# Moving the last output projection of an RWKV-7 layer behind the operands of the next stage

## The chip, the cores and the metric

The kernel runs on one core of a Trainium2 chip. The metric is the device time of one execution in microseconds (us). A core has five engines that run their own instruction streams side by side: TensorE (PE, matrix products, with the weight load shown apart as PEld), VectorE (DVE), ScalarE (ACT), GpSimd (POOL) and SyncE (SP, which here only issues transfers). PE writes its results to PSUM; all other data of the engines lies in SBUF, and transfers (DMAs) carry it to and from the chip's memory (HBM). A DMA is issued from the queue of SP, ACT or POOL. Each engine and each queue works in its own fixed order; an instruction that waits holds up what stands behind it.

## The reference

One inference step of a two-layer trunk with width 1024, for 1024 prompt tokens and 8 x 16 sample tokens (1152 columns in all). Layer 0 is RWKV-7 time mixing and a SwiGLU FFN, layer 1 is chunk-band attention with shared keys and values and a SwiGLU FFN. What matters here is the end of the time mixing of layer 0 and the entry into its FFN:

```python
y = ((y - mu) * lax.rsqrt(var + LNX_EPS)).reshape(bsz, t, d)      # per head of 64
y = y * ln_w + ln_b
y = y + bonus                                                     # r, k, v of the same token
out = (y * g) @ w_o                                               # the output projection
...
x = x + gt_m[:, None, :] * out                                    # the residual
h = modulate(rms_norm(x, p['norm_ffn'][l]), sh_f, sc_f)           # the FFN's input
x = x + gt_f[:, None, :] * swiglu(h, w_gate, w_up, w_down)
```

The norm's factor of a token, rsqrt(mean of x squared), needs all 1024 features of the new x, so all eight output tiles of the projection.

## The kernel before, in words

Data lies with features on the 128 partitions (8 feature tiles) and tokens along the free axis. Every float32 product is done as three products of a high and a low part: `split` (L268, L269) makes them, the high part with a copy on ACT, the low part with a subtraction on DVE; `mm3` issues the three matmuls (all by `mm`, L139).

Layer 0 works on three blocks of 384 tokens (`NB`, `TB`). Each block's projections run for all features; then its tokens go through the recurrence in *windows* of 128 tokens, three per block, each in two halves `hf` of four feature tiles. Window w of block b is (w, hf) with b = w // 3. Windows 6, 7 and 8 belong to block 2; window 8 holds the sample tokens. `win_run` computes a half window, `win_y` collects its result in one PSUM bank, and `win_post` (L1047 on) ends it: loads of the gate (tile gl, L1052) and of the bonus (bv, L1054), the copy out of PSUM (y, L1056), the per-head norm by two matmuls with constants and ACT's Square (L1059), Ln (L1063) and Exp (L1064), three DVE steps (L1065, L1069, L1070), and a store to the DRAM tensor yg of the block from ACT's queue (L1071). gl, bv and y have one buffer each.

`outproj(b)` is the output projection of a block. It loads the block's yg feature by feature on SP's queue (tile mr, two buffers, L1166), splits it into 16 operand tiles (tag mx), and then for each of 8 output tiles takes a weight tile (`wunit`: load of rw_o, two buffers, on POOL's queue by `wload` at L256, then a split of 1024 columns into whi and wlo), runs 24 matmuls of 384 columns into one of two PSUM banks, adds the gated result to x (`residual`, L1151 to L1156), stores it to the DRAM tensor x1 (L1179) and adds its squares to a sum (`sq_add`, L306 and L307). At the end `sq_done` makes the factors (one matmul with ones, `rsqrt2`, L326 to L330), and they are stored to the DRAM tensor rr (L1182).

`layer0a` runs the windows of block 2 in the order (6,0) (6,1) (8,0) (7,0) (7,1) (8,1), two at a time, and beside them the projections of blocks 0 and 1. After the last window its pool of buffers is closed, and `outproj(2)` follows.

`dense` is the rest. It opens two pools where the windows' pool was: h0 (14 tiles of 1024 columns, tag h) and wq (16 tiles of 512 columns, tag w, and five, tag rq). The FFN's tokens are two groups, c = 0 (tokens 0 to 511, all from blocks 0 and 1) and c = 1 (tokens 512 to 1151, with all of block 2). A group's gate and up products use Strassen's scheme: `strassen_in` loads the factors (L1438) and the eight input tiles (L1262), applies norm and shift (`normed`, L349 and L350, for sample tokens L357 to L359), forms 16 sums of a half width (256 or 320 columns, `comb`, L1268, on GpSimd) and splits 28 half tiles. Its inputs for c = 0 lie for the time being in w tiles, those for c = 1 in a pool (tag e) that takes the place of the projection's operand tiles. `strassen_weights` loads four weight tiles into rq tiles, forms four sums (L1309 to L1312), and splits seven. `gate_up` multiplies, sums with DVE and GpSimd (L1338), and stores; `ffn` runs it for the first weight tile on c = 0 and on c = 1 apart, and for the 21 others on both.

The order of instructions on each engine is not written out by hand: the program is emitted in the order of the code, and a scheduler in the build simulates the program's time and puts each engine's and each queue's instructions in order by which can start, the earlier emitted first where several can. The order is fixed from then on. A tile in a newly opened pool waits for the older tiles that lay on its bytes, each tile by itself.

Of the kernel before, what the change touches and what calls it, by code (L numbers as in the profile page):

```python
# [17 lines left out]
TB = 384  # L18
# [123 lines left out]
class Trunk:  # L142
# [166 lines left out]
    def sq_done(self, st):  # L309
# [9 lines left out]
        r = self.ev("rms", 1)[:, :w]  # L319
# [726 lines left out]
    def win_post(self, w, hf, R):  # L1046
# [4 lines left out]
        gt = self.wt("gl", [128, 512], 1)  # L1051
        nc.sync.dma_start(gt.rearrange("p (f t) -> p f t", f=4), self.sp[b]["g"][:, wi, fs, :])  # L1052
        bv = self.wt("bv", [128, 512], 1)
        nc.sync.dma_start(bv.rearrange("p (f t) -> p f t", f=4), self.sp[b]["v"][:, wi, fs, :])  # L1054
        y = self.wt("y", [128, 512], 1)
# [15 lines left out]
        nc.scalar.dma_start(self.yg[b][:, fs, wi * 128:(wi + 1) * 128], y.rearrange("p (f t) -> p f t", f=4))  # L1071
# [85 lines left out]

    def outproj(self, b):
# [3 lines left out]
        hi, lo = [], []  # L1162
        for f in range(8):
            h, l = self.mtile(), self.mtile()
            t = self.mraw()
            nc.sync.dma_start(t, self.yg[b][:, f, :])  # L1166
            self.split(h, l, t)
            hi.append(h)
            lo.append(l)
# [12 lines left out]
        nc.sync.dma_start(self.rr[:, cols], self.sq_done(st))  # L1182

    def layer0a(self, ctx):
        self.yg = [self.dp.tile([128, 8, TB], F32, name=f"yg{b}") for b in range(NB)]
# [16 lines left out]
        def early():  # L1202
            yield from self.alternate(self.outproj(0), self.ada, 1, 1)
            yield from self.outproj(1)
        for _ in self.alternate(self.windows([divmod(int(x), 2) for x in '12 13 16 14 15 17'.split()]), early(), 1, 2):
            pass
        cw.close()
        for _ in self.outproj(2):
            pass
        self.wqueue = None  # L1210
# [5 lines left out]
    def wide_open(self, ctx, name):  # L1216
        self.wq = ctx.enter_context(self.tc.tile_pool(name="wq" + name, bufs=1, reuse_waits="tile"))
        self.rawtag = "h0"
        self.hw = ("w", "w", 16)
        self.halfraw = lambda: self.wq.tile([128, 512], F32, tag="rq", name=self.nm("rq"), bufs=5)  # L1220

# [33 lines left out]
    def strassen_in(self, B, x, r, A, sh0, c, X):  # L1255
# [4 lines left out]
        gp = nc.gpsimd  # L1260
# [162 lines left out]
    def dense(self, x2, x3, close):  # L1423
# [4 lines left out]
        with ExitStack() as ctx:  # L1428
            pool = lambda n, **k: ctx.enter_context(self.tc.tile_pool(name=n, bufs=1, reuse_waits="tile", **k))
            self.hps = {0: pool("h0")}  # L1430
            with ExitStack() as c2:
                self.wide_open(c2, "0")
# [3 lines left out]
                def part(c, temp):  # L1436
                    r, *X = [temp() for _ in range(9)]
                    nc.sync.dma_start(r, self.rr[:, self.cols(c)])  # L1438
                    return self.strassen_in(B, self.x1, r, A, 24, c, X)
# [513 lines left out]
```

## Time and profile before

| | |
|---|---|
| median of 3 runs | 3858.28 us (3854.87 to 3863.27) |
| the profiled execution | 3864.46 us |
| its span, first to last instruction | 3862.7 us |
| granted PE clock over the span | 0.932 of full speed |
| instructions | 72343 |

The profile belongs to one execution. Its times count from the span's start. A row of the order of time gives start, length, engine, line, operation, and the tiles as output<-input with their shapes; in brackets stands how long the engine was idle before it, and what ended that. Releasers are inferred from semaphores. A row of a group gives the number of instructions, their busy time in us, the mean of one in ns and the idle time before them. The clock that the throttle granted to PE is a share of full speed. The stretch that the change touches lies between about 1200 and 1400 us.

### The profile page before, as it was taken

Reading aid. Unit: us, or ns where it says so; the run is one execution under the profiler, and the core shown is the slowest. Engines: PE = TensorE matmul, PEld = TensorE weight load, DVE = VectorE, ACT = ScalarE, POOL = GpSimd, SP = SyncE. Lnnn points to the kernel's source line nnn. Section 1 sums busy time; section 2 is a strip of 40 time slices with the busy share of each in tenths; the row PEclk is TensorE's granted clock in tenths of the full one; section 3 lists DMA queues with packets and bytes.
Section 4 is the critical chain, followed back from the end, with each engine's and each line's share of the span. In section 5 each row is a group of like instructions: output and inputs, shape, how many; then the busy total and the mean of one; then the engine's idle time right before and its main releaser. Section 6 shows DMA issues by size and latency. Waiting matters only on the chain.

```text
span 3862.7 us, 72343 instructions
## 1 busy us (share of the span) xinstructions
PE 3540.6 (92%) x28614; PEld 3125.0 (81%) x28614; DVE 2291.8 (59%) x4420; ACT 1575.7 (41%) x2998; POOL 643.2 (17%) x564
## 2 busy tenths in 40 slices
PE   5889989989888699999999899789889799999999
PEld 4777778777666599999887879677777799999998
DVE  4666666765445764554456752666675764554567
ACT  5545646544223433333311353565654533333310
POOL 0000000000010364453000100000000254453000
PEclk8887998889798789999999999899999899999999
DMA  5775776776664412223755112454555322222521
GB/s 209 233 218 163 214 207 182 200 199 199 187 201 147 143 67 75 74 75 105 254 179 182 70 62 97 141 152 140 153 185 167 116 80 75 74 75 92 171 86 70
DMA packets 428963, 552.31 MB, mean 143 GB/s; under 512 B 128432, under 2 KB 296880, under 8 KB 424144
## 3 DMA queue, kind: packets, MB, share of 16 engines
q1 hardware_dynamic: 352640, 449.49, 36.4%
q0 software_dynamic: 21840, 79.31, 6.8%
q10 hardware_dynamic: 54144, 18.89, 2.1%
q8 instruction: 225, 3.69, 0.4%
q14 instruction: 114, 0.93, 0.1%
HBM read 413.42 MB, written 134.12 MB: 142 GB/s over the span
## 4 chain that ended last, share of the span: by engine, by line
PE 69%; DMA 9%; DVE 9%; issue 6%; ACT 5%; POOL 1%; SPq 1%; ACTq 0%; DVEq 0%; POOLq 0%
PE S L139 31%; PE PT L139 15%; PE acc L139 13%; PE st L139 3%; PE O L139 2%; PE G L139 1%; DVE h L269 1%; PE PT L1779 1%; PE aux L139 1%; DMA raw<-in_wada 1%; DMA TT<-Z 1%; DMA Z<-T 1%; DVE wlo L269 1%; PE Y L139 1%; ACT pts L1780 1%
## 5 line engine op out<-in xcount | busy, mean ns | idle before, releaser
L139 PE MATMUL S<-h,w 128*128 128x320 f32 (+1 forms) x4944 | 698.9, 300 | 18.2 <-DVE h L269 7.7
L139 PEld LDWEIGHTS S<-h,w 128*128 128x128 f32 x4944 | 676.8, 192 | 26.6 <-DVE h L269 12.8
L139 PE MATMUL acc<-mx,whi 128*128 128x384 f32 x1728 | 512.5, 374 | 41.8 <-ACT mx L268 20.2
L139 PE MATMUL S<-h,wh 128*128 128x320 f32 (+1 forms) x2844 | 529.8, 337 | 14.0 <-DVE h L1151 8.1
L139 PEld LDWEIGHTS S<-h,wh 128*128 128x128 f32 x2844 | 455.4, 189 | 70.6 <-issue 11.7
L139 PEld LDWEIGHTS acc<-mx,whi 128*128 128x128 f32 x1728 | 340.4, 205 | 74.1 <-ACT mx L268 23.9
L268 ACT ACTIVATE w<-rq 128x512 fp32r<-128x512 f32 x308 | 192.4, 629 | 503.5 <-PE S L139 203.1
L269 DVE TENSOR_TENSOR w<-rq,w 128x512 fp32r<-128x512 f32 x308 | 268.6, 875 | 199.5 <-ACT w L268 198.9
L139 PE MATMUL PT<-h,w 128*128 128x320 f32 (+1 forms) x2448 | 355.4, 300 | 14.1 <-ACT w L268 6.9
L139 PEld LDWEIGHTS PT<-h,w 128*128 128x128 f32 x2448 | 337.9, 192 | 17.8 <-ACT w L268 7.1
L139 PE MATMUL acc<-mx,wlo 128*128 128x384 f32 x864 | 318.8, 369 | 6.5 <-DVE wlo L269 6.5
L139 PE MATMUL PT<-h,wh 128*128 128x320 f32 (+1 forms) x1428 | 286.4, 344 | 10.8 <-DVE wh L269 3.9
L1338 POOL TENSOR_TENSOR t<-t,t 128x576 f32<-128x576 f32 (+1 forms) x132 | 216.5, 1641 | 417.0 <-ACT t L1345 295.3
L139 PEld LDWEIGHTS PT<-h,wh 128*128 128x128 f32 x1428 | 233.5, 190 | 41.7 <-issue 6.0
L269 DVE TENSOR_TENSOR wlo<-raw,whi 128x1024 fp32r<-128x1024 f32 x114 | 139.6, 1226 | 85.3 <-ACT whi L268 84.3
L139 PEld LDWEIGHTS acc<-mx,wlo 128*128 128x128 f32 x864 | 176.7, 205 | 16.3 <-DVE wlo L269 10.3
L269 DVE TENSOR_TENSOR h<-h,h 128x1024 fp32r<-128x1024 f32 (+4 forms) x112 | 122.9, 1111 | 89.9 <-ACT h L268 73.0
L268 ACT ACTIVATE wh<-rq 128x512 fp32r<-128x512 f32 x124 | 74.8, 625 | 242.8 <-PE S L139 160.7
L268 ACT ACTIVATE h<-h 128x1024 fp32r<-128x1024 f32 (+4 forms) x112 | 103.3, 935 | 168.1 <-DMA h<-sd 111.7
L268 ACT ACTIVATE whi<-raw 128x1024 fp32r<-128x1024 f32 x114 | 119.6, 1053 | 124.3 <-PE acc L139 78.9
L1338 DVE TENSOR_TENSOR t<-S,t 128x576 f32<-128x576 f32 (+1 forms) x116 | 86.4, 745 | 132.0 <-PE S L139 132.0
L1405 DVE TENSOR_TENSOR h<-h,S 128x640 f32<-128x640 f32 (+1 forms) x150 | 111.9, 750 | 78.8 <-PE S L139 78.7
(433 smaller groups left out, 5754.7 us busy)
## 6 DMA issues: line engine op xcount, KB each, us to landing
h<-in_wada SPq DMA_DIRECT2D x64, 512.0 KB, 6.4
rq<-in_wg SPq DMA_DIRECT2D x88, 256.0 KB, 2.6
rq<-in_wu SPq DMA_DIRECT2D x88, 256.0 KB, 2.6
rq<-in_wd SPq DMA_DIRECT2D x88, 256.0 KB, 3.0
raw<-in_wada POOLq DMA_DIRECT2D x32, 512.0 KB, 5.0
kc<-in_ck SPq DMA_DIRECT2D x16, 1024.0 KB, 5.0
vc<-in_cv SPq DMA_DIRECT2D x16, 1024.0 KB, 5.8
sd<-t SPq DMA_DIRECT2D x88, 160.0 KB, 1.9
```

What stands on the lines that cost most here:

```text
L139: return nc.tensor.matmul(out, lhsT, rhs, start=start, stop=stop)
L268: self.nc.scalar.activation(hi, x, AF.Copy)
L269: self.nc.vector.tensor_tensor(lo, x, hi, ALU.subtract)
L1338: eng.tensor_tensor(out, x, y, ALU.add)
L1405: nc.vector.tensor_tensor(y, y, d, ALU.add)
L1779: nc.tensor.transpose(pt[:, j * 128:(j + 1) * 128], P[:, j * 128:(j + 1) * 128], self.C("ident"))
L1780: nc.scalar.activation(pts[:, 0:nk * 128], pt[:, 0:nk * 128], AF.Copy)
```

## The change

- `win_post`: the half window (7, 1) takes its gl, bv and y from the ring TT (six buffers of the same size) instead of the three single buffers. The half windows (7, 1) and (8, 1) no longer store y to yg: each splits its four 128-column pieces directly into the columns of the operand tiles of `outproj(2)`.
- `last_in` and `out_in`: the operand tiles of `outproj(2)` are made once, right after `outproj(1)` or with the first of these two ends. Their loads go through `wload`, at that time on POOL's queue, and for features 4 to 7 only the first 128 of 384 columns (window 6) are loaded.
- `dense`: the operands of group c = 0 are emitted ahead of `outproj(2)`; `outproj(2)` then alternates with the making of the first FFN weight tiles, four steps to one.
- The norm factors of block 2 stay in an SBUF tile (r2, one of the five rq tiles); group c = 1 copies them from there with ACT, and loads only the 256 factors of block 1 from rr.
- In layer 0 the sums of `strassen_in` for both groups run on VectorE instead of GpSimd. Layer 1 keeps them on GpSimd.
- `wide_open` is divided, so that the pool wq can be open while `outproj(2)` still takes its raw weights from the projection's pool.

```diff
-    def sq_done(self, st):
+    def sq_done(self, st, r=None):
...
-        r = self.ev("rms", 1)[:, :w]
+        r = self.ev("rms", 1)[:, :w] if r is None else r
...
-        gt = self.wt("gl", [128, 512], 1)
+        new = lambda tag: self.wt(tag, [128, 512], 1)
+        if (w, hf) == (7, 1):
+            new = lambda tag: self.wt("TT", [128, 8, 64], 6).rearrange("p c t -> p (c t)")
+        gt = new("gl")
...
-        bv = self.wt("bv", [128, 512], 1)
+        bv = new("bv")
...
-        y = self.wt("y", [128, 512], 1)
+        y = new("y")
...
-        nc.scalar.dma_start(self.yg[b][:, fs, wi * 128:(wi + 1) * 128], y.rearrange("p (f t) -> p f t", f=4))
+        if hf == 1 and w > 6:
+            cs = slice(wi * 128, (wi + 1) * 128)
+            for f in range(4):
+                h, l = (t[4 + f][:, cs] for t in self.last_in())
+                self.split(h, l, y[:, f * 128:(f + 1) * 128])
+        else:
+            nc.scalar.dma_start(self.yg[b][:, fs, wi * 128:(wi + 1) * 128], y.rearrange("p (f t) -> p f t", f=4))
+
+    def last_in(self):
+
+        if not self.yin:
+            self.yin = self.out_in(2, self.wload, 128)
+        return self.yin
...
-    def outproj(self, b):
-
-        nc, pp = self.nc, self.pp
-        cols = slice(b * TB, (b + 1) * TB)
+    def out_in(self, b, load, n=TB):
+
         hi, lo = [], []
         for f in range(8):
             h, l = self.mtile(), self.mtile()
-            t = self.mraw()
-            nc.sync.dma_start(t, self.yg[b][:, f, :])
-            self.split(h, l, t)
+            m = TB if f < 4 else n
+            t = self.mraw()[:, :m]
+            load(t, self.yg[b][:, f, :m])
+            self.split(h[:, :m], l[:, :m], t)
             hi.append(h)
             lo.append(l)
+        return hi, lo
+
+    def outproj(self, b):
+
+        nc, pp = self.nc, self.pp
+        cols = slice(b * TB, (b + 1) * TB)
+        hi, lo = self.last_in() if b == 2 else self.out_in(b, nc.sync.dma_start)
...
-        nc.sync.dma_start(self.rr[:, cols], self.sq_done(st))
+        if b < 2:
+            nc.sync.dma_start(self.rr[:, cols], self.sq_done(st))
+        else:
+            self.r2 = self.halfraw()[:, :TB]
+            self.sq_done(st, self.r2)
...
             yield from self.outproj(1)
+            self.last_in()
...
         cw.close()
-        for _ in self.outproj(2):
-            pass
-        self.wqueue = None
...
-    def strassen_in(self, B, x, r, A, sh0, c, X):
+    def strassen_in(self, B, x, r, A, sh0, c, X, gp=None):
...
-        gp = nc.gpsimd
+        gp = gp or nc.gpsimd
...
                 def part(c, temp):
                     r, *X = [temp() for _ in range(9)]
-                    nc.sync.dma_start(r, self.rr[:, self.cols(c)])
-                    return self.strassen_in(B, self.x1, r, A, 24, c, X)
+                    if c:
+                        nc.sync.dma_start(r[:, 0:256], self.rr[:, 512:768])
+                        nc.scalar.activation(r[:, 256:640], self.r2, AF.Copy)
+                    else:
+                        nc.sync.dma_start(r, self.rr[:, self.cols(c)])
+                    return self.strassen_in(B, self.x1, r, A, 24, c, X, nc.vector)
...
+                W = []
+
+                def weights():
+                    for t in self.strassen_weights(0, 0, nc.vector):
+                        W.append(t)
+                        yield
                 for _ in part(0, lambda: self.wq.tile([128, 512], F32, tag="w", name=self.nm("x"), bufs=16)):
                     pass
-                W = list(self.strassen_weights(0, 0, nc.vector))
+                for _ in self.alternate(self.outproj(2), weights(), 4, 1):
+                    pass
+                self.wqueue = None
+                self.rawtag = "h0"
                 close()
```

More of the change, by code (lines that the diff above doesn't have):

```diff
@@ L1156, in residual @@
             nc.vector.tensor_tensor(out[:, n:], t, x[:, n:], ALU.add)
+    def out_in(self, b, load, n=TB):
+        hi, lo = [], []
+        for f in range(8):
+            h, l = self.mtile(), self.mtile()
+            m = TB if f < 4 else n
+            t = self.mraw()[:, :m]
+            load(t, self.yg[b][:, f, :m])
+            self.split(h[:, :m], l[:, :m], t)
+            hi.append(h)
+            lo.append(l)
+        return hi, lo
     def outproj(self, b):
@@ L1161, in outproj @@
         cols = slice(b * TB, (b + 1) * TB)
-        hi, lo = [], []
-        for f in range(8):
-            h, l = self.mtile(), self.mtile()
-            t = self.mraw()
-            nc.sync.dma_start(t, self.yg[b][:, f, :])
-            self.split(h, l, t)
-            hi.append(h)
-            lo.append(l)
+        hi, lo = self.last_in() if b == 2 else self.out_in(b, nc.sync.dma_start)
         st = self.sq_open()
@@ L1181, in outproj @@
             yield
-        nc.sync.dma_start(self.rr[:, cols], self.sq_done(st))
+        if b < 2:
[3 more added lines that the diff above has]
+            self.sq_done(st, self.r2)
     def layer0a(self, ctx):
+        self.yin = None
         self.yg = [self.dp.tile([128, 8, TB], F32, name=f"yg{b}") for b in range(NB)]
@@ L1207, in layer0a, with wq_open, wide_open @@
         cw.close()
-        for _ in self.outproj(2):
-            pass
-        self.wqueue = None
         ct.push(c1)
         return ct.close
-    def wide_open(self, ctx, name):
+    def wq_open(self, ctx, name):
         self.wq = ctx.enter_context(self.tc.tile_pool(name="wq" + name, bufs=1, reuse_waits="tile"))
-        self.rawtag = "h0"
         self.hw = ("w", "w", 16)
         self.halfraw = lambda: self.wq.tile([128, 512], F32, tag="rq", name=self.nm("rq"), bufs=5)
+    def wide_open(self, ctx, name):
+        self.wq_open(ctx, name)
+        self.rawtag = "h0"
     def wide_open2(self, ctx, name):
@@ L1431, in dense @@
             with ExitStack() as c2:
-                self.wide_open(c2, "0")
+                self.wq_open(c2, "0")
                 A = self.gain("nf0", 32)
@@ L1447, in done @@
                     yield from self.normed_split(c, *X[c], self.Ak, 96, *HK[c])
+                W = []
[3 more added lines that the diff above has]
+                        yield
                 for _ in part(0, lambda: self.wq.tile([128, 512], F32, tag="w", name=self.nm("x"), bufs=16)):
                     pass
-                W = list(self.strassen_weights(0, 0, nc.vector))
+                for _ in self.alternate(self.outproj(2), weights(), 4, 1):
+                    pass
+                self.wqueue = None
+                self.rawtag = "h0"
                 close()
```

## The prediction, on record before the changed kernel was run

> **What bounds the kernel now.** I read the page first, then the busy time by stage around the place that the change touches, then who waited there, then the instructions in order of time.
>
> ```profile
> span 3862.7 us, 72343 instructions
> PE 3540.6 (92%) x28614; PEld 3125.0 (81%) x28614; DVE 2291.8 (59%) x4420; ACT 1575.7 (41%) x2998; POOL 643.2 (17%) x564
> ```
>
> TensorE (PE) is busy for 92% of the span, so over the whole kernel only its idle stretches and its slow ones can be won. The view by stage shows one such place, about 130 us long (columns: the stretch, its length, then busy us and instructions of PE, of PE's weight load, of VectorE, ScalarE and GpSimd, then the granted clock, DMA share, GB/s).
>
> ```profile
> 1240.00:1262.00 22.00, 4.30 (x8) 1.05 (x6) 5.09 (x13) 3.40 (x7) 0.00 (x0) 0.55 0.24 71
> 1262.00:1316.00 54.00, 39.87 (x168) 35.94 (x168) 47.18 (x84) 29.17 (x59) 22.62 (x20) 0.80 0.47 155
> ...
> 1330.00:1372.00 42.00, 31.25 (x120) 24.63 (x119) 37.79 (x68) 21.52 (x46) 28.48 (x24) 0.63 0.23 80
> 1372.00:1400.00 28.00, 28.00 (x200) 28.00 (x201) 18.35 (x25) 11.00 (x20) 15.54 (x13) 0.94 0.29 98
> ```
>
> The first stretch is the end of the last two windows: every engine is nearly idle. The second is the last output projection (168 of its 192 matmuls; 24 ran earlier) together with the first group's operands: VectorE (DVE) is busy 47.18 of 54 us, and PE works at a granted clock of 0.80. The third is the second group's operands: DVE 37.79 of 42 us, PE at 0.63. From 1372 PE is dense. So this place is bound first by a chain of waits and then by DVE. The order of time shows the chain (start, length, engine, line, what; the idle time before it and its releaser in brackets), first PE, then ScalarE (ACT).
>
> ```profile
> 1238.83 1.30 PE L139 MATMUL Y<-XL,ssv 64*64 64x16 f32 x30
> ...
> 1261.97 1.33 PE L139 MATMUL acc<-mx,whi 128*128 128x384 f32 x3 [9.42 <-ACT mx L268]
> ```
>
> ```profile
> 1242.94 0.43 ACTq L1071 DMA_DIRECT2D yg<-y  x1
> 1247.06 0.60 ACT L1056 ACTIVATE y<-Y 128x512 f32<-128x512 f32 x1 [6.78 <-DMA yg<-y]
> ...
> 1256.59 0.37 ACTq L1071 DMA_DIRECT2D yg<-y  x1
> 1261.39 1.02 ACT L268 ACTIVATE mx<-mr 128x384 fp32r<-128x384 f32 x2 [7.46 <-DMA mr<-yg]
> ```
>
> Window 8's result is complete in PSUM at 1240.13 (1238.83 + 1.30), but its copy starts only at 1247.06, since window 7's end has the one buffer y until its store is out. The end itself then takes 9.5 us (1247.06 to the store at 1256.59), and another 5.4 us go by (1256.59 to 1261.97) while y is written to memory, read back and split.
>
> **The change part by part.**
>
> **(1) The last ends.** Window 7's end takes three buffers of another ring, so window 8's copy can follow its matmuls at 1240.2; both ends write their split straight into the projection's operand tiles. That removes two stores on ACT's queue and cuts four loads to a third of their columns.
>
> ```profile
> L269 DVE TENSOR_TENSOR h<-x,h 128x256 fp32r<-128x256 f32 x28 | 15.3, 574 | 2.0 <-ACT h L268 1.9
> ...
> L349 DVE SCALAR_TENSOR_TENSOR x<-x,mod,x 128x512 f32<-128x512 f32 x8 | 5.8, 749 | 2.2 <-DMA x<-x 2.2
> L307 DVE TENSOR_TENSOR sqa<-sqa,kk 128x384 f32<-128x384 f32 x7 | 5.6, 800 | 1.7 <-ACT kk L306 1.7
> ...
> L1156 DVE TENSOR_TENSOR e<-e,rr 128x128 f32<-128x128 f32 x8 | 2.3, 282 | 0.1
> ...
> L269 DVE TENSOR_TENSOR mx<-mr,mx 128x384 fp32r<-128x384 f32 x4 | 2.2, 557 | 5.4 <-ACT mx L268 5.4
> ```
>
> (DVE's groups from 1262 to 1322: busy us, mean ns, idle before.) In place of 4 splits of 384 columns, 2.2 us on DVE, stand 12 of 128, at 0.28 us as a sum of that width: 3.4 us, and only window 8's first is on the path. An ACT split of 128 columns has no row; it lies below the 0.52 us (1.02 for two) of 384, so PE starts at 1240.2 + 9.5 + 0.5 = 1250.2 at the latest instead of 1261.97: **11.8 us**. The eight loads that are left move from SP's queue to GpSimd's (POOL), among the weight loads:
>
> ```profile
> raw<-in_rw_o POOLq DMA_DIRECT2D x8, 512.0 KB, 4.0
> x<-x SPq DMA_DIRECT2D x8, 320.0 KB, 6.4
> x<-e SPq DMA_DIRECT2D x12, 192.0 KB, 2.0
> ...
> mr<-yg SPq DMA_DIRECT2D x8, 192.0 KB, 3.1
> ```
>
> ```profile
> 1211.77 1.39 SPq L1166 DMA_DIRECT2D mr<-yg  x2
> ```
>
> A POOL load lands after 4.0 us, an SP load after 3.1. With two buffers the eight make four rounds, so some 4 us are added in all, and there are more than 35 us between the first issue now (1211.77) and 1250: hidden. If one of them waits for an operand tile at the head of POOL's queue, weight loads stand behind it, and PE waits for those: 4 us then. The Trainium skill (SBUF — State Buffer, section on the two separate sides) speaks against this move: the descriptors of a GpSimd load cannot be written while VectorE holds the port pair that the two share. The 4.0 us were measured beside a busy DVE, and no run here shows the small loads on this queue; by the rule they would land later still, inside the same 35 us.
>
> **(2) First group's operands ahead of the last projection.** Nine loads on SP, 8 norms, 28 splits and 16 sums are emitted before the projection instead of after it, so they go first where both are ready; the projection's weight splits and residuals, and the FFN's first seven weight tiles (now one for every fourth step) queue behind them on DVE and ACT.
>
> ```profile
> 1194.84 0.55 DVE L307 TENSOR_TENSOR sqa<-sqa,kk 128x384 f32<-128x384 f32 x1
> ...
> 1274.17 0.41 DVE L269 TENSOR_TENSOR h<-x,h 128x256 fp32r<-128x256 f32 x1
> ...
> 1329.69 0.29 DVE L357 TENSOR_TENSOR x<-x,x 128x128 f32<-128x128 f32 x1 [7.32 <-DMA x<-x]
> ...
> 1335.65 0.48 DVE L269 TENSOR_TENSOR h<-x,h 128x320 fp32r<-128x320 f32 x1
> ...
> 1353.09 12.70 DVE L269 TENSOR_TENSOR h<-x,h 128x320 fp32r<-128x320 f32 x11
> ```
>
> A split takes 0.41 us where POOL is still and 0.574 on the mean of this stretch, the sum of squares 0.55 against 0.80. Putting the 16 sums on DVE, each taken as a split of that width, adds 16 x 0.41 = 6.6 us and gives back 28 x 0.164 + 7 x 0.25 = 6.3 us: even. So DVE's work stays at about 47.5 us, and what counts is how much of it goes into the hole before 1250, in which DVE is now nearly idle. By the code, though, the operands' buffers lie where the windows' buffers were: an input whose place window 7's end now uses can be loaded only after that end (about 1243) and must then land, and the first h tile waits the same way for window 8's y. I put 5 us of the work ahead of 1250.2 (bounds: 0, and 21, all norms and splits). The remaining 42.5 us, with DVE 92% busy (87% now), take 46 us: the projection's last matmul ends at 1296 instead of 1316.25 (the residual of it, below): **20 us** with (1) in it. The bounds: the stretch keeps its 54.3 us (1261.97 to 1316.25), which leaves the 11.8 of (1); or PE alone sets it, at its fast pace. Four rows of the chain:
>
> ```profile
> 1201.54 4.20 PE acc L139 x24
> ...
> 1316.28 0.48 DVE e L1151
> ...
> 1321.81 0.57 DVE rms L330
> ...
> 1322.40 3.38 DMA rr<-rms
> ```
>
> 168 matmuls at 4.20 us for 24 are 29.4 us, the end 1279.6, the gain 36.7.
>
> **(3) Norm factors kept.** Now the factors are ready at 1322.38, go to memory (3.38 us), and only then does SP fetch them and, behind them, the inputs; the first norm (L357) starts at 1329.69, 13.4 us after the last matmul.
>
> ```profile
> L306 ACT ACTIVATE kk<-e 128x384 f32<-128x384 f32 x7 | 3.7, 523 | 10.0 <-DVE e L1156 10.0
> ```
>
> One ACT copy of 384 columns, 0.52 us as a square of that width, stands in for the round trip, and the input loads no longer stand behind it: they wait for the projection's operand tiles, whose place they take, and for x1, so all but the last can be issued from the last matmul on. The first norm starts at 1323 by the old clock: **7 us**. Bounds: 0, if the last store and the loads (2.0 and 6.4 us to land, above) come last all the same, and 7. The kept tile holds one of five weight buffers until that copy; the FFN's sixth temporary needs it later: nothing.
>
> **(4) Second group's sums on DVE.** 11 splits that ran beside POOL took 12.70 us (above), 1.15 each, against 0.48 alone. DVE's splits from 1322 to 1372, then POOL's sums:
>
> ```profile
> L269 DVE TENSOR_TENSOR h<-x,h 128x320 fp32r<-128x320 f32 x27 | 22.7, 884 | 1.8 <-ACT h L268 1.8
> ```
>
> ```profile
> L1268 POOL TENSOR_TENSOR x<-x,x 128x320 f32<-128x320 f32 x12 | 13.6, 1144 | 2.4 <-DVE h L269 2.4
> ...
> L1268 POOL TENSOR_TENSOR x<-x 128x320 f32<-128x320 f32 x4 | 4.3, 1066 | 0.1
> ```
>
> POOL loses 17.9 of its 28.5 us here, 63%. DVE's splits now lose 27 x (0.884 - 0.48) = 10.9 us to POOL; 63% of it is 6.9 us given back, against 16 x 0.48 = 7.7 us added. That is even on DVE; but splits and PE no longer wait for POOL's chain. I take **2 us** (bounds: 7.7 us lost if nothing is given back; 8 us won if the sums fall into DVE's 4.2 us of idle time as well and the rest of the 10.9 shrinks with it). POOL's other additions stay. By the same page of the Trainium skill GpSimd and a VectorE instruction with two inputs shut each other out for the whole instruction; the rows agree, 1.15 us being one POOL sum of 1.07 to 1.14. By it each POOL sum removed frees its full time, 17.9 - 7.7 = 10 us, and the time would be about 3821.
>
> The sum is 20 + 7 + 2 = 29 us. The profiled execution took 3864.46 us, 1.8 us more than its span; 29 less is 3835.5. The median of the runs, 3858.28, is 6.2 us below that execution, so I forecast **3829 us**.
>
> **The rivals.** *Operands no earlier.* The input loads now run at 1260.38, right behind the projection's own:
>
> ```profile
> 1259.02 0.80 SPq L1166 DMA_DIRECT2D mr<-yg  x2
> ...
> 1260.38 1.80 SPq L1262 DMA_DIRECT2D x<-x  x4
> ```
>
> If they are issued no sooner, for want of free buffers, only (1) and (3) are won, less up to 5 us for PE waiting behind the operands: 14 to 19, about 3842. For it: the shared places. Against it: most of the inputs lie where buffers of the solves and of earlier windows were, done long before.
>
> *PE waits behind the operands: slower.* The place is DVE's queue after 1250. If all of the first group's work stands ahead of the six weight splits that are left, PE has nothing from about 1258 until the group is done, and then needs 6 x 4.20 = 25 us, some 6 us of slow clock, and 6.1 us from the last matmul to the factors.
>
> ```profile
> 1305.10 0.41 DVE L269 TENSOR_TENSOR h<-x,h 128x256 fp32r<-128x256 f32 x1
> ```
>
> If the group ends no earlier than now (its last splits, above), the factors come at 1342 instead of 1322.4; less 9 from (3) and (4) that is 11 us slower, 3869. It decides from 1294 on (1322.4 + 9 - 37). Against it: DVE's 28 us for the group (15.3 + 5.8 + 6.6) would have to stretch to 44 from 1250, and now the two kinds of work interleave.
>
> *No change that counts.* (1) and (3) hold, but the added sums cost their upper bound in both groups (6.6 + 7.7 = 14.3 us) and nothing is given back: 11.8 + 7 - 14.3 = 4.5 us won, 3854. Against it: 0.41 against 0.574, and 0.48 against 0.884.
>
> *More than forecast.* POOL's sums free their full time, or most operands are done in the hole: 43 us, 3815.
>
> **How the numbers follow.** Forecast (20 to 39 us won) 0.52; operands no earlier (8 to 20) 0.22; more than forecast 0.11; no change that counts 0.08; slower 0.07. A difference under 0.2%, 7.7 us, cannot be told from none here. Faster by more: 0.52 + 0.22 + 0.11 = 0.85; within: 0.08; slower: 0.07. The range goes from 49 us won, just short of all the best bounds (36.7 + 7 + 8 = 52), to 7 us won: 3809 to 3851, leaving out 0.15 above and about 0.03 below.
>
> **What would show it.** PE's first matmul of the rest of the projection should come about 10 us after the last matmul of Y, not 21.8; the projection's last one 46 us later; DVE's first norm of the second group 7 us after that, not 13.4; POOL has no L1268 sums before the second layer; and the dense stretch begins near 1343, not 1372. Step (2) is wrong if the first group's norms start after 1260; step (4) if splits of 320 columns still average over 0.7 us. The forecast fails as a whole if PE stands idle for more than 15 us at a time between 1250 and 1300, or if the windows before 1210 or the stages after the dense stretch begins change their length by more than 10 us.

## The result, and the profile after

The changed kernel takes 3833.27 us (median of five runs, 3832.17 to 3838.13), the kernel before, run beside it, 3863.27 us (five runs, 3854.87 to 3876.49). The ratio is 0.9926, its 95% interval 0.991 to 0.9941: 23 to 35 us faster. The forecast was 3829 us, range 3809 to 3851. The profiled execution took 3837.45 us, against 3864.46 before: 27.0 us less.

The head of the page of the changed kernel:

```profile
span 3835.7 us, 72353 instructions
...
PE 3523.0 (92%) x28614; PEld 3116.7 (81%) x28614; DVE 2288.2 (60%) x4460; ACT 1574.6 (41%) x3007; POOL 618.9 (16%) x540
```

The totals hardly move: VectorE issues 40 instructions more and is busy 3.6 us less, GpSimd 24 fewer. So the place itself must be read. The view by stage of the changed kernel, in the columns of the prediction (the first two rows are stretches that the prediction shows of before; the dense stretch now begins at 1350):

```profile
1240.00:1262.00 22.00, 13.68 (x40) 9.31 (x38) 13.24 (x33) 10.53 (x24) 0.00 (x0) 0.58 0.44 145
1262.00:1316.00 54.00, 42.13 (x223) 39.45 (x223) 48.15 (x117) 31.29 (x67) 3.53 (x5) 0.86 0.43 139
1296.00:1350.00 54.00, 31.82 (x173) 28.16 (x172) 40.84 (x102) 28.41 (x60) 18.19 (x8) 0.78 0.33 108
1350.00:1400.00 50.00, 50.00 (x379) 50.00 (x378) 28.71 (x33) 16.79 (x28) 28.40 (x19) 1.00 0.21 71
```

In the first row PE is busy 13.7 us where it was 4.3: the rest of the projection starts there. In the second, VectorE is busy for 48.15 us where it was 47.18, but runs 117 instructions where it ran 84, and GpSimd 3.5 us where it had 22.6. The order of time on PE in the changed kernel shows the edges of the stages:

```profile
1239.75 0.80 PE L139 MATMUL Y<-XL,ssv 64*64 64x16 f32 x7
...
1250.60 1.33 PE L139 MATMUL acc<-mx,whi 128*128 128x384 f32 x3 [4.41 <-ACT mx L268]
...
1296.49 0.34 PE L139 MATMUL acc<-mx,wlo 128*128 128x384 f32 x1
1301.03 1.53 PE L139 MATMUL aux<-sqa,cst 128*128 128x384 f32 x2 [4.20 <-DVE sqa L307]
...
1345.42 1.17 PE L139 MATMUL S<-h,w 128*128 128x320 f32 x3 [8.73 <-ACT t L1372]
```

Y is complete at 1240.55, the rest of the projection starts 10.1 us later (21.8 before) and ends at 1296.83, 46.2 us later (54.3 before). Those are the numbers forecast (10, 46). The last row was not forecast: 8.73 us of idle PE in the second group.

For all that follows I use one length: from the end of Y to SP's first store of the third full group of FFN half tiles, the first "sd" store that lies wholly in dense work. It covers all four parts of the change and leaves out the windows ahead and the attention behind. Before, then after:

```profile
1420.49 3.16 SPq L1359 DMA_DIRECT2D sd<-t  x4
```

```profile
1396.66 3.16 SPq L1386 DMA_DIRECT2D sd<-t  x4
```

That is 1420.49 - 1240.13 = 180.4 us before and 1396.66 - 1240.55 = 156.1 us after: 24.2 of the 27.0 us were won here. "The stretch" below is this length.

### The profile page after: what moved, and what is told of

Read it like the earlier page. It is cut to its first block, busy times and chain, and to the rows that moved or that the text cites. A ratio compares the mean times of both kernels' runs of the same rounds, so it can differ in the third digit from the quotient of the medians.

```text
span 3835.7 us, 72353 instructions
## 1 busy us (share of the span) xinstructions
PE 3523.0 (92%) x28614; PEld 3116.7 (81%) x28614; DVE 2288.2 (60%) x4460; ACT 1574.6 (41%) x3007; POOL 618.9 (16%) x540
## 3 DMA queue, kind: packets, MB, share of 16 engines
q8 instruction: 225, 3.69, 0.4%
## 4 chain that ended last, share of the span: by engine, by line
PE 70%; DMA 10%; DVE 10%; issue 5%; ACT 4%; POOL 1%; SPq 1%; ACTq 0%; DVEq 0%; POOLq 0%
PE S L139 32%; PE PT L139 15%; PE acc L139 12%; PE st L139 3%; PE O L139 2%; DVE h L269 1%; PE PT L1819 1%; PE G L139 1%; PE aux L139 1%; PE Y L139 1%; DMA TT<-Z 1%; DMA raw<-in_rw_o 1%; DMA raw<-in_wada 1%; DVE wlo L269 1%; DMA Z<-T 1%
## 5 line engine op out<-in xcount | busy, mean ns | idle before, releaser
L139 PE MATMUL S<-h,w 128*128 128x320 f32 (+1 forms) x4944 | 690.6, 298 | 25.9 <-ACT t L1372 8.7
L139 PE MATMUL PT<-h,wh 128*128 128x320 f32 (+1 forms) x1428 | 286.4, 344 | 10.6 <-DVE wh L269 4.6
```

Of the source, the lines that this page charges most:

```text
L139: return nc.tensor.matmul(out, lhsT, rhs, start=start, stop=stop)
```

## The experiments

Each kernel ran beside the kernel before, whose medians in these later runs were 3860.84 to 3867.05 us; each ratio goes by its own. The times of whole runs scatter by 10 us and more for one and the same kernel, so the stages of the profiled executions carry the argument. In the table: PE's restart after the end of Y, the length of the rest of the projection, from its last matmul to the second group's first norm, the stretch, the median, and the ratio to before with its interval.

| kernel | restart | projection | to norm | stretch | median us | ratio (95%) |
|---|---|---|---|---|---|---|
| before | 21.8 | 54.3 | 13.4 | 180.4 | 3863.27 | |
| changed | 10.1 | 46.2 | 9.2 | 156.1 | 3833.27 | 0.9926 (0.991-0.9941) |
| changed, again | 10.4 | 47.3 | 7.8 | 157.4 | 3840.74 | 0.9939 (0.9919-0.996) |
| (1) alone | 10.2 | 52.4 | 12.8 | 165.3 | 3854.9 | 0.9978 (0.9963-0.9994) |
| (1)+(4) | 9.9 | 42.0 | 18.2 | 161.8 | 3846.05 | 0.994 (0.9915-0.9966) |
| (1)+(3)+(4): old order | 9.9 | 40.3 | 10.4 | 153.3 | 3839.7 | 0.9946 (0.9929-0.9963) |
| (1)+(2)+(4): factors by memory | 10.4 | 46.5 | 14.1 | 162.8 | 3851.95 | 0.9962 (0.9943-0.9981) |
| (1)+(2)+(3): sums on GpSimd | 10.0 | 53.0 | 6.7 | 159.2 | 3843.73 | 0.9962 (0.9949-0.9975) |
| changed, weight sums on VectorE | 10.3 | 44.8 | 9.4 | 147.1 | 3829.09 | 0.9919 (0.9904-0.9934) |
| the same, other buffers | 9.9 | 48.0 | 7.5 | 148.4 | 3838.4 | 0.9935 (0.9914-0.9955) |
| old order, weight sums | 10.4 | 40.0 | 10.6 | 146.0 | 3827.55 | 0.9905 (0.9884-0.9926) |
| old order, weight sums, input | 10.4 | 40.1 | 9.6 | 145.1 | 3824.57 | 0.9883 (0.9859-0.9908) |
| new order, weight sums, input | 10.1 | 44.7 | 8.8 | 146.4 | 3825.81 | 0.9888 (0.9867-0.9909) |

**Does the stretch repeat?** The changed kernel, unaltered.

> The changed kernel once more, unaltered: how far do its stages repeat? Measured from the end of Y (last matmul of the last window) to the first store of the third group of half tiles in the FFN, a stretch that covers all four parts of the change: 180.4 us before, 156.1 after. If the last projection and the two operand groups are what moved, this stretch repeats within 2 us, while the windows ahead of it (Y ended at 1240 to 1251 in the runs so far) and the attention stage behind it (531.6 to 539.9) wander by several us in any kernel; then the 5 us that came on top in the attention stage are nothing of the change. If the attention stage is at 531.6 again, they belong to the changed program.

It repeats within 1.3 us (156.1 and 157.4), so differences of 3 us and more are read as such, smaller ones are not. That rests on one pair, since no other kernel was profiled twice. Its parts repeat about as well (46.2 and 47.3 us for the projection, 9.2 and 7.8 to the norm). Outside it things wander: Y was complete at anything from 1231.9 to 1251.1 us in these kernels. The attention stage, from the first matmul of the next projection's split weights (row 1 of each pair) to GpSimd's first operand sum of the second layer (row 2), in the order of time of the kernel before, the changed kernel, and the changed kernel again:

```profile
2477.24 0.80 PE L139 MATMUL acc<-h,wh 128*128 128x256 f32 x2 [8.76 <-ACT wh L268]
...
3013.88 4.38 POOL L1268 TENSOR_TENSOR h<-h,h 128x256 f32<-128x256 f32 x3 [177.54 <-DMA vf<-in_wo]
```

```profile
2454.34 0.79 PE L139 MATMUL acc<-h,wh 128*128 128x256 f32 x2 [10.36 <-ACT wh L268]
...
2985.89 3.93 POOL L1295 TENSOR_TENSOR h<-h,h 128x256 f32<-128x256 f32 x3 [173.24 <-DMA vf<-in_wo]
```

```profile
2449.52 0.79 PE L139 MATMUL acc<-h,wh 128*128 128x256 f32 x2 [9.63 <-ACT wh L268]
...
2987.53 3.93 POOL L1295 TENSOR_TENSOR h<-h,h 128x256 f32<-128x256 f32 x3 [175.10 <-DVE h L269]
```

536.6, 531.6, 538.0 us. The 5.1 us that the first profile of the changed kernel had won in the attention stage are gone in the second: they are not the change's.

**Step (1) alone.** The kernel before, with `last_in` and `out_in` of the change and

```diff
+        if (w, hf) == (7, 1):
+            new = lambda tag: self.wt("TT", [128, 8, 64], 6).rearrange("p c t -> p (c t)")
...
+        if hf == 1 and w > 6:
+            ... self.split(h, l, y[:, f * 128:(f + 1) * 128])
```

> The kernel before with step (1) alone: window 7's end on buffers of its own, both last ends splitting straight into the projection's operands; order, factors and GpSimd sums as before. By my sum 11.8 us: PE's rest of the projection starts 10 us after the end of Y, not 21.8, the projection keeps its 54 us, and the stretch from the end of Y to the third group's first store is 168 to 169 us instead of 180.4. Rival: the idle time ahead of the projection was no loss, since VectorE then has the same work in a shorter time: the projection's matmuls stretch from 54 to 60 us and more, and the stretch is 174 to 180.

The restart comes 10.2 us after Y, and the stretch falls from 180.4 to 165.3: 15.1 us, 3 more than expected. The rival is out: the projection did not stretch, it took 52.4 us, 1.9 less.

The loads that moved to GpSimd's queue, which the prediction held against this step, did not land later. In the changed kernel the eight are issued from 1212.66 to 1227.75 and land after 2.0 to 2.8 us, where those on SP's queue took 3.1.

**Step (4): the sums, one group seen against the other.** First with the new order, the changed kernel with

```diff
-                    return self.strassen_in(B, self.x1, r, A, 24, c, X, nc.vector)
+                    return self.strassen_in(B, self.x1, r, A, 24, c, X)
```

> The changed kernel (profiled 3837.45 us) with the 2 x 16 operand sums of the first FFN layer back on GpSimd: term (4) alone is undone. By my sum the second group's operands take 2 us longer than with the sums on VectorE, so the dense stretch begins about 2 us later than 1350.35 (and a few us more by the first group's stretch, whose splits slow down again from 0.41 to 0.57 us). By the reading of the trace after, the move lost about 2 us: from the first norm of the second group to the dense stretch it took 42.1 us before and 44.3 after, since GpSimd's own sum for the next weight tile took 8.64 us instead of 1.3 beside VectorE's unbroken row of two-input instructions, and PE waited 8.73 us for what follows it; with the sums back on GpSimd the 320-column splits are at 0.9 us again, and this part takes 42 us again. Whole kernel then: 3837 +- 3 us, no difference. Third theory, by the Trainium skill (SBUF - State Buffer, two separate sides): each GpSimd sum shuts VectorE out for its whole length, 17.9 us here, so this kernel is some 10 us slower.

The projection takes 53.0 us with the sums on GpSimd and 46.2 with them on VectorE. From the last matmul to the store it is the other way round: 159.2 - 63.0 = 96.2 us on GpSimd, 156.1 - 56.3 = 99.8 on VectorE. Together the move gains 2.4 us (against the mean of the two runs of the changed kernel), which is less than the 3 us from which a difference is read. Of the 3.6 us lost, 2.5 lie ahead of the first norm (6.7 us and 9.2; 7.8 when the changed kernel ran again) and 1.1 behind it (89.5 us from the norm to the store, and 90.6; 91.9 again). None of the three expectations fits: the first has the sign of the second group wrong, the second leaves out the first group, and the third, the 10 us by the Trainium skill (SBUF — State Buffer, section on the two separate sides), is four times too large. VectorE's groups between 1250 and 1306, of the kernel with the sums on GpSimd, then of the changed kernel (busy us, mean ns of one, idle before):

```profile
L269 DVE TENSOR_TENSOR h<-x,h 128x256 fp32r<-128x256 f32 x28 | 16.7, 631 | 0.5 <-ACT h L268 0.5
```

```profile
L269 DVE TENSOR_TENSOR h<-x,h 128x256 fp32r<-128x256 f32 x28 | 10.5, 409 | 0.0
...
L1295 DVE TENSOR_TENSOR x<-x,x 128x256 f32<-128x256 f32 x12 | 4.9, 408 | 0.0
...
L1295 DVE TENSOR_TENSOR x<-x 128x256 f32<-128x256 f32 x4 | 1.6, 409 | 0.0
```

In these groups VectorE's time is even, as the prediction said: 16.7 us against 10.5 + 4.9 + 1.6 = 17.0. Over the whole projection it is busy for 45.7 us with the sums on GpSimd and for 42.1 with them on VectorE (43.0 when run again). The waits differ more. ScalarE, then VectorE, then PE, in the order of time of the kernel with the sums on GpSimd:

```profile
1274.84 0.42 ACT L268 ACTIVATE h<-x 128x256 fp32r<-128x256 f32 x1 [5.62 <-POOL x L1295]
1275.17 1.04 ACT L268 ACTIVATE whi<-raw 128x1024 fp32r<-128x1024 f32 x1
```

```profile
1280.43 5.74 DVE L269 TENSOR_TENSOR h<-x,h 128x256 fp32r<-128x256 f32 x4
```

```profile
1290.23 0.98 PE L139 MATMUL acc<-mx,whi 128*128 128x384 f32 x2 [7.84 <-ACT w L268]
```

One GpSimd sum that is late holds an operand split at the head of ScalarE's queue for 5.62 us, and the projection's weight split stands behind it. Some 5 us later four VectorE splits take 5.74 us, and PE stands for 7.84 us. The row puts that down to ScalarE's w by inference; what the matmul needs last is its bank, which VectorE's residual behind those splits frees at 1290.09. Its raw weights are late too: their load stands among the sums in GpSimd's order, is issued at 1281.93 and can be split from 1286.03. With the sums on VectorE both chains lose their third engine.

Then in the old order, against (1) alone: (1) and (4), with the `nc.vector` above, the projection ahead of the operands, and the factors through memory.

> Steps (1) and (4) alone: the last ends, and the first layer's 32 operand sums on VectorE; old order, factors through memory. Against the kernel with the ends alone (52.4 us for the projection, 165.3 from the end of Y to the third group's first store) it shows the sums by themselves in the old order. Theory: what I put down to the order, a shorter projection, comes from the sums: without GpSimd beside it a split of the first group takes 0.41 us and not 0.63, and the projection takes 40 to 42 us; part of it is given back in the second group, where GpSimd's weight sum starves, and the stretch is 159 to 161. Rival: the kept factors did it in the runs so far (with them and the old order 40.3 and 153.3): then the projection is at 50 or more and the stretch at 163 to 166.

The projection falls from 52.4 to 42.0 us: the sums by themselves do it, and the rival is out. But the stretch gains only 3.6 us (165.3 to 161.8). From the last matmul to the store it takes 161.8 - 51.9 = 109.9 us, against 165.3 - 62.6 = 102.7: 7.2 of the 10.4 are given back. Most of that is no loss of the second group, since 5.3 us lie ahead of its first norm (18.2 us against 12.8). VectorE at the end of the projection, in the order of time of (1) and (4):

```profile
1291.14 1.08 DVE L269 TENSOR_TENSOR h<-x,h 128x256 fp32r<-128x256 f32 x3
...
1295.30 0.47 DVE L1166 SCALAR_TENSOR_TENSOR e<-acc,mod,rr 128x256 f32<-128x256 f32 x1
```

The last matmul ends at 1291.14, and VectorE comes to its residual (L1166) only at 1295.30, after splits of the first group's operands and weights; in (1) alone 0.04 us lie between. The projection ends sooner, with more of the first group's work left over. Behind the first norm 1.8 us are lost (91.7 us against 89.9). So from the end of Y to the first norm the move gains 5.4 us in the old order (75.4 to 70.1) and 4.2 in the new (69.7 to 65.5).

**What the second group loses.** The changed kernel with

```diff
-            self.gate_up(sd[f // 2][:, f % 2], B, self.strassen_weights(l, f), (0, 1))
+            self.gate_up(sd[f // 2][:, f % 2], B, self.strassen_weights(l, f, nc.vector if (l, f) == (0, 1) else None), (0, 1))
```

> The changed kernel with the four kinds of sums of the FFN's second weight tile (12 products, tile 1) on VectorE instead of GpSimd; tile 0 has its sums there already. Theory: PE's 8.73 us of idle time at 1336.7 to 1345.4 comes from GpSimd, starved for 8.64 us in one sum, and from ScalarE's queue, where three operand splits stand behind the weight's split that waits for it. Then this wait goes, and the dense stretch begins 5 to 8 us earlier (1342 to 1345 instead of 1350.35), the kernel at 3830 to 3832 in its profiled execution. Rival: VectorE sets the pace there anyway, and the sums that it now takes itself (about 2.5 us) come on top: the dense stretch begins at 1350 to 1353, the idle time of PE is put down to VectorE's splits, the kernel the same or 2 us slower.

The stretch is 147.1 us, 9.1 to 10.3 less than the two runs of the changed kernel: the theory holds, and its size was put too low. The chain in the changed kernel, first GpSimd, then ScalarE in the order of time:

```profile
1330.85 8.64 POOL L1336 TENSOR_TENSOR rq<-rq,rq 128x512 f32<-128x512 f32 x1 [7.67 <-DVE h L269]
1339.56 1.26 POOL L1337 TENSOR_TENSOR rq<-rq,rq 128x512 f32<-128x512 f32 x1
1340.90 1.26 POOL L1338 TENSOR_TENSOR rq<-rq,rq 128x512 f32<-128x512 f32 x1
1342.24 1.26 POOL L1339 TENSOR_TENSOR rq<-rq,rq 128x512 f32<-128x512 f32 x1
```

```profile
1343.54 0.63 ACT L268 ACTIVATE w<-rq 128x512 fp32r<-128x512 f32 x1 [9.84 <-POOL rq L1339]
1344.07 0.45 ACT L268 ACTIVATE h<-x 128x320 fp32r<-128x320 f32 x1
...
1345.79 0.46 ACT L268 ACTIVATE h<-x 128x320 fp32r<-128x320 f32 x1
...
1346.90 0.45 ACT L268 ACTIVATE h<-x 128x320 fp32r<-128x320 f32 x1
```

Four sums of one shape on one engine: the first takes 8.64 us, the others 1.26. The first runs beside a VectorE that is working without a gap; VectorE in the same stretch of the changed kernel:

```profile
1337.48 0.88 DVE L269 TENSOR_TENSOR h<-x,h 128x320 fp32r<-128x320 f32 x2
1344.20 0.69 DVE L269 TENSOR_TENSOR w<-rq,w 128x512 fp32r<-128x512 f32 x1 [5.83 <-ACT w L268]
```

It has two-input instructions one after the other until 1338.36, and GpSimd's sum is done at 1339.49. Then VectorE itself stands idle for 5.83 us behind ScalarE, whose queue has a weight split at its head that waits for GpSimd's fourth sum, with three operand splits and the copy of a product (t, L1372, which PE's row names) behind it, and PE has nothing for 8.73 us. Before the change GpSimd was itself a member of VectorE's chain: VectorE waited for GpSimd's operand sums, and GpSimd's other sums got in between. With the operand sums gone, VectorE no longer stops.

With the weight sums on VectorE, its splits of the second group take 481 ns as in the changed kernel (VectorE's group from 1300 to 1345), and PE's largest idle time in that group is 2.5 us (its row in the order of time):

```profile
L269 DVE TENSOR_TENSOR h<-x,h 128x320 fp32r<-128x320 f32 x28 | 12.8, 481 | 0.1
```

```profile
1329.10 0.41 PE L139 MATMUL S<-h,w 128*128 128x320 f32 x1 [2.48 <-ACT h L268]
```

From the first norm to the store it takes 82.6 us, 8.0 to 9.3 less than in the two runs of the changed kernel, and 6.9 less than with all of these sums on GpSimd (89.5). Moving the operand sums is a gain there, which the starved weight sums take back.

**Step (2): the order.** The changed kernel with

```diff
+                for _ in self.outproj(2):
+                    pass
                 for _ in part(0, ...):
                     pass
-                for _ in self.alternate(self.outproj(2), weights(), 4, 1):
+                for _ in weights():
                     pass
```

> The changed kernel with the last output projection emitted ahead of the first group's operands and the first weight tile again: only the order of step (2) is undone; own tiles at the last ends, kept factors and the sums on VectorE stay. My theory: PE starts the rest of the projection at about 1250 as after the change (step (1)), but the stretch keeps nearly its old 54 us less what the sums on VectorE save: the projection's last matmul ends at 1302 to 1305 instead of 1296.8, and the kernel is 5 to 8 us slower than the changed one, 3843 to 3846 profiled. Rival: the order counts for nothing, since both kinds of work share VectorE, which needs the same time for them in any order: the first group's operands, then ready, come out late instead, the projection ends earlier (1285 to 1290), the dense stretch begins at 1350 +- 3, and the kernel is the same.

The edges on PE in the order of time of this kernel:

```profile
1241.88 2.14 PE L139 MATMUL Y<-XL,ssv 64*64 64x16 f32 x40
...
1253.94 1.33 PE L139 MATMUL acc<-mx,whi 128*128 128x384 f32 x3 [4.41 <-ACT mx L268]
...
1293.89 0.34 PE L139 MATMUL acc<-mx,wlo 128*128 128x384 f32 x1
```

Y is complete at 1244.02, and the projection runs from 1253.94 to 1294.23. The order that the prediction held to be the gain is none: with the old one the projection takes 40.3 us, not 46.2, and the stretch 153.3, 2.8 to 4.1 less. The rival has it, and is still a little too kind to the new order. For the same 168 matmuls PE is busy for 34.3 us at a granted clock of 0.93 with the old order, and for 38.6 us at 0.82 with the new; what lowered the clock was not tested. The medians (3839.7 here, 3833.27 and 3840.74 for the changed kernel) can't tell the two apart. In both orders the first group's first norm comes behind the last window's end, 10.8 us after Y with the new order and 12.5 with the old: nothing of the first group went into the hole ahead of PE's restart. VectorE in the order of time of the changed kernel:

```profile
1247.62 0.69 DVE L1068 TENSOR_TENSOR y<-st,y 128x512 f32<-128x512 f32 x1 [3.69 <-ACT y L1067]
...
1250.58 0.90 DVE L269 TENSOR_TENSOR mx<-y,mx 128x128 fp32r<-128x128 f32 x4 [0.38 <-ACT mx L268]
1251.40 2.07 DVE L349 SCALAR_TENSOR_TENSOR x<-x,mod,x 128x512 f32<-128x512 f32 x3
```

It stands idle for 3.69 us in the hole, but the norms (L349) stand behind window 8's end in its order, and follow that end at once. With the new order the first group's splits then only stand ahead of the projection's own on VectorE and ScalarE.

The same with the GpSimd stall taken out, to see whether it hides the order's worth:

> The changed kernel with two edits: the old order (projection first, then the first group's operands and weights), and the second weight tile's sums on VectorE. Theory from the runs so far: the order costs 2.8 us in the stretch from the end of Y to the third group's first store (153.3 with the old order against 156.1), and the starved GpSimd sum 9.1 (147.1 with that tile on VectorE); together, where PE's idle 5.5 us behind ScalarE's split go in the old order too, the stretch is 144 to 148 us and the kernel at 3820 to 3828 profiled. Rival: the new order is the better one by 6 us, as the medians of the runs say (3839.7 against 3833.27), and the stretch is 150 or more, the kernel at 3831 or more.

146.0 us, against 147.1 with the new order: equal within what repeats. The theory's size fits (144 to 148), the rival does not.

**The buffers of window 7's end.** The changed kernel with the weight sums, and

```diff
-            new = lambda tag: self.wt("TT", [128, 8, 64], 6)...
+            new = lambda tag: self.wt("pa", [128, 2, 8, 64], 1)[:, 0]... if tag == "y" else self.wt("Aab", [128, 8, 64], 2)...
```

> The changed kernel with two edits: the second weight tile's sums on VectorE, and window 7's end on buffers of another kind (two of the four-buffer ring of the solves' sums and the half of one scan tile) in place of three of the ring whose place three of the first group's inputs take. My step (2) said that these inputs wait for that end; in the trace after, SP's queue stood 9.2 us at them (1237.95 to 1247.1) and VectorE had 4.1 us of idle time at 1253.5. If that wait costs what it seems to, the first group's norms start before 1250 and the stretch from the end of Y to the third group's first store is 142 to 145 us, against 147.1 with the weight sums alone. Rival: VectorE is busy for 36.7 of the next 38 us and sets the pace of that stretch whatever is done early, other places (the first h tile, window 8's y) hold the rest up: 147 +- 1.5.

148.4 us against 147.1: no gain, as the rival has it. The input loads still stand on SP's queue for 7.53 us (9.17 in the changed kernel), and the first norm still comes 10.7 us after Y. So those three places were not what held the first group up. Here too the first norm follows window 8's end on VectorE without idle time; why it was put behind that end was not tried.

**Step (3): the factors.** The changed kernel with the factors written to memory and read back:

```diff
-        if b < 2:
-            nc.sync.dma_start(self.rr[:, cols], self.sq_done(st))
-        else:
-            self.r2 = self.halfraw()[:, :TB]
-            self.sq_done(st, self.r2)
+        nc.sync.dma_start(self.rr[:, cols], self.sq_done(st))
```

> The changed kernel with the last block's norm factors sent through memory again: only step (3) is undone. The second group's inputs are then queued behind the load of the factors again. By my sum 7 us: the first norm of the second group comes 13 to 16 us after the projection's last matmul instead of 9.2, and the dense stretch begins 7 us later (1357). By the reading of the trace after, in which the factors were ready 8.6 us after the last matmul and not 6.1 because the last residual waited for its input, and the first norm came 0.6 us behind the copy: also 6 to 7 us later (factors 8.6, store 3.4, load 2 or more, against 0.5 for the copy). Rival: since the group's pace is set by what comes behind (GpSimd's starved sum, VectorE's work), the later norms are caught up: dense stretch at 1350 to 1353 and the kernel within 2 us.

14.1 us to the first norm, and the stretch 162.8: 5.4 to 6.7 us longer. The rival, by which the later norms are caught up, is out. In the old order, between the rows with and without it, 161.8 - 153.3 = 8.5. The 7 us of the prediction lie between.

**Two versions that beat both kernels.** The last residual in the changed kernel waits for its input, whose load waits for a buffer. Both kernels with the weight sums on VectorE got one edit more, `x = self.ev("rms", 1) if (b, f) == (2, 7) else self.ev("rr")`: the last input goes into the buffer that the kept factors leave free.

> The kernel with the old order and the second weight tile's sums on VectorE (146.0 us in the stretch), and one edit more: the last residual's input goes into the one factor buffer that the kept factors leave free, so its load need not wait for the residual two before it. If the last residual waits for its input only (0.6 us seen in the trace) the first matmul of the norm comes 2.8 to 3.3 us after the projection's last one, not 3.6, and the stretch is 145 to 146; profiled 3818 to 3828, and at least as fast as the changed kernel by more than the interval. Rival: the last residuals wait for PE and VectorE alone: 3.6 again.

> The same two edits (weight sums of the second tile on VectorE, the last residual's input in a free buffer) on the changed kernel's own order: 147.1 us in the stretch without the second. The last residual waited 0.4 us for its input and the norm's first matmul came 4.2 us after the last of the projection. Expected 2.5 to 3.5 and a stretch of 145.5 to 147. Beside the kernel with the old order it says whether the order of step (2) is worth anything once GpSimd's stall is gone: my prediction says that it is the faster one; the runs so far say equal within 1.5 us.

The norm's first matmul comes 2.75 us after the last of the projection instead of 3.6 (old order), and 3.7 instead of 4.2 (new): half a microsecond to one. The 2.5 to 3.5 us expected for the new order were not reached, and the second profile of the changed kernel has 2.6 us without the edit, so this gain is not shown. The stretches, 145.1 and 146.4, stay within what repeats of those without the edit. The medians are 3824.57 and 3825.81 us, with ratios of 0.9883 (0.9859 to 0.9908) and 0.9888 (0.9867 to 0.9909): both intervals lie below both of the changed kernel's. The gain over the changed kernel is that of GpSimd's weight sums, 9 to 10 us.

## Why the prediction was right, and where it was not

The forecast of 3829 us was 4 us off the median, and 29 us of gain stand against 24.2 in the stretch. The whole profiled execution won 27.0: the attention stage's 5.1 are wander, and the rest of the program lost 2.3. From row to row of the table the parts are (1) 15.1, (4) 3.6, (3) 8.5, (2) -2.8; they add up to 24.2 by construction, which proves none of them. The total was right, and two of the four reasons. That the errors nearly cancelled is luck.

- **(1), 11.8 us: right, and mis-sized by 3.** The restart at 1250.2 came at 1250.60. The rest is that the projection itself got 1.9 us shorter and the second group a little; the prediction had no term for that.
- **(1) and (2) together, 20 us; the projection's last matmul at 1296.** It came at 1296.83, but for another reason. The step that failed reads: "what counts is how much of it goes into the hole before 1250", with 5 us put ahead of PE's restart. None was: the first norm began at 1251.40. With the order undone the projection ends earlier after Y, 50.2 us against 56.3; with the sums on GpSimd it takes 53.0 us in the new order, against 52.4 with (1) alone. VectorE's 42.5 us for this stretch were met (42.1), but not because work had moved ahead of it: with the sums on GpSimd they are 45.7. What I named as the sign of failure, norms after 1260, was too weak to show it; the length of the projection with the order alone undone does.
- **The sums in the first group, "even": right for VectorE's groups (16.7 us against 17.0), wrong as a step.** They shorten the projection by 6.7 us in the new order and by 10.4 in the old, and the way from Y to the first norm by 4.2 and 5.4. The chain from VectorE to GpSimd and on to ScalarE was set by its waits, 5.62 us on ScalarE and 7.84 on PE, since the weight splits and residuals that PE needs stand behind them. The prediction had seen this for the second group ("splits and PE no longer wait for POOL's chain") and not for the first. At the edge of 1296 two errors, one on each side, cancelled: 8.2 us given to the order (20 less 11.8), and none to the sums.
- **(3), 7 us: right.** 5.4 to 8.5 by the runs. The first norm came 9.2 us after the last matmul, not 7, because the last residual started 1.9 us after that matmul: VectorE was at the tile before until 1298.36, and then waited 0.41 us for its input.
- **(4), 2 us for the second group: not won.** Behind the first norm the move lost 1.1 to 2.4 us in the new order and 1.8 in the old, too little to be read as a loss. The mark that I named, splits of 320 columns under 0.7 us, was met at 0.48, and did not show it. The step that failed is the sentence "POOL's other additions stay", priced at nothing: the prediction asked what GpSimd costs VectorE, and not what a VectorE without gaps costs GpSimd. That is worth 9 to 10 us, as the run without those sums shows. By the Trainium skill (SBUF — State Buffer, section on the two separate sides) whichever of the two starts first has the shared port pair for its whole instruction and the other waits; the trace agrees that they shut each other out, and shows the side that the prediction left out, 8.64 us for a sum of 1.26. The time that I worked out from that rule, 3821, was not met (3833.27), nor was it with the weight sums on VectorE as well (3829.09).
- **The rivals.** "Operands no earlier" was right about its mechanism, none of the work went into the hole, and wrong about its price, since that work was not where the gain lay. "PE waits behind the operands" has the direction of the order alone, which costs at most 3 to 4 us and not 11.
- **The signs.** The dense stretch began at 1350, forecast 1343: the 7 us are GpSimd's stall. With the weight sums on VectorE it begins at 1342.

## What to carry to other kernels

Before work moves off an engine, ask what its waits did for the others: taking GpSimd out of VectorE's chain made that chain fast and left the rest of GpSimd's work without a turn. Here, moving the rest of the work that is wanted soon as well won 9 to 10 us more. Busy time that comes out even did not show what a chain over three engines would gain; price its hand-overs, and what stands behind the waiting instruction on each in-order queue. And a sum whose total is met is no proof of its terms: only undoing each part showed that the reordering won nothing.

## What was not expected of the hardware

A GpSimd sum of 128x512 beside an unbroken row of two-input VectorE instructions did not get its turn between two of them: it took 8.64 us against 1.26 and ended 1.1 us after the row did. It took 8.51 us when the kernel ran again, 7.75 with the old order and 9.90 in (1) and (4), and each time ended 1.1 us after the row; with GpSimd's sums in the same chain as VectorE's splits the same sum took 1.52 us. GpSimd, in the order of time of the kernel with the sums on GpSimd:

```profile
1337.99 1.52 POOL L1336 TENSOR_TENSOR rq<-rq,rq 128x512 f32<-128x512 f32 x1
```

Where the waiting GpSimd stands in the choice between the two engines was not measured beyond this.
